# A two-layer decoder trunk on one core: where the overflow test stands, and how the last expert's last products are cut, gated and summed

## The chip, the core and the metric

The kernel runs on one core of a Trainium2 chip. The metric is device time in microseconds (us) of one execution; the median of several executions is compared. The core's engines are TensorE (PE in the profile; its weight loads are PEld), VectorE (DVE), ScalarE (ACT), GpSimd (POOL) and SyncE (SP). Here SP issues the weight loads, which 16 DMA engines carry out. Each engine works through its own queue of instructions in order and waits on semaphores for the others.

## The reference, cut to what matters

Two layers, each a token mixer and a channel mixer, with layer norms. 256 tokens, 1024 channels, float32. What the change touches is the last sub-layer: eight experts of width 3584, of which each token uses its best two, and the final layer norm.

```python
def moe_swiglu(x, w_router, w_gate_up, w_down):
    logits = (x @ w_router).astype(jnp.float32)
    top_v, top_i = lax.top_k(logits, TOP_K)
    gates = jax.nn.softmax(top_v, axis=-1)
    combine = jnp.sum(jax.nn.one_hot(top_i, N_EXPERTS, dtype=jnp.float32) * gates[..., None], axis=-2)
    y = jnp.zeros_like(x)
    for e in range(N_EXPERTS):
        y = y + combine[..., e:e + 1].astype(x.dtype) * swiglu(x, w_gate_up[e], w_down[e])
    return y
...
h = layer_norm(DEEPNORM_ALPHA * h + f, ln_ffn_g[l], ln_ffn_b[l])
```

## The kernel before

**Places and slots.** Only the rows that an expert really gets are computed. The experts are ordered by their load at run time (place 0 has the most tokens), and each place has a fixed number of slots: `SLOTS = [192, 128, 128, 64, 64, 32, 32, 32]`. A place's tokens are gathered by a product with a one-hot matrix (`gather`), run through the expert as slots, and sent back to tokens by a product with the transposed one-hot matrix (`back`). The result is multiplied by the token's gate and added to `acc` (256 x 1024, as two tiles of 128 tokens), which starts as the scaled residual.

**Overflow.** If an expert gets more tokens than its place has slots, a block under `tc.If(most > 0)` (`overflow`, L1629 to L1637, which calls `rest`) computes the others. Every engine evaluates the test; with the inputs used here the block isn't entered.

**Two chains.** `big` runs places 0, 1 and 2 with weights split into a high and a low part (ACT makes `whi` at L433, DVE `wlo` at L434, and PE multiplies in the fast fp32r format). `small` runs places 7, 6, 5, 4, 3 with raw fp32 weights, several slot groups side by side in the PE array (`Packed`). `merge` interleaves the two chains' steps by the counts in `MERGE`; the loop over `both_chains()` counts the steps as `n` and does other things at given steps. Each expert has up steps (gate and up projections) and then down steps. A down step of the small chain takes two loads of 1 MB, each with two k tiles of 128 rows by 1024 columns.

**Loads.** `slot` takes the next of `RING = 8` buffers of 1 MB and issues the load on SP (L389). SP's queue is in order, so a load waits for its buffer to be free, and all later loads wait behind it. `value_load` (L1515) reads an expert's number into a register of SP.

**The end before.** The last expert is place 3 (64 slots; the 128 rows of a bank hold two halves of 64, each a partial sum over different columns or k tiles). In its down steps (`plain_job.downs`), at `i == BRANCH` (2), six loads (`LEAD`) are issued ahead, then the overflow test is made, then the rest follows. Of its last two 1 MB loads, the left 512 columns of both come as one load and the right 512 columns as two of half the size. `last` (L219 to L251) multiplies them, copies the slot sums from PSUM with ACT (`last_y`, L216), sends them back to tokens in fp32 in four banks, and for each bank DVE multiplies by the gate and adds to `acc` (L238) and takes statistics (L514). PE's order there is written out by hand. Then DVE alone makes the final norm: mean and variance (L1590), the inverse root in small steps (L520 to L527) with four cells of 512 columns normalised between them (L1599), four last steps of 512 columns (L1601), each followed by its output DMA (L1602).

PSUM has eight banks here: four `mm`, two `tp`, two `aux`. Instructions of ACT, DVE and SP are ordered by the framework's own simulated timeline unless an order is written out, and it can't move anything into or across the block of the overflow test.

Of the kernel before, what the change touches and what calls it, by code (L numbers as in the profile page):

```python
# [23 lines left out]
NE = 8  # L24
# [55 lines left out]
class Packed:  # L80
# [5 lines left out]
    half = [slice(0, 64), slice(64, 128)]  # L86
# [126 lines left out]
    def last_y(self, bank):  # L213

        y = self.b.pp.tile([128, 512], F32, name="y", tag="gfar", bufs=3)
        self.nc.scalar.activation(y, bank, AF.Copy)  # L216
        return y

    def last(self, keys, ws, st):  # L219


        nc, b, half = self.nc, self.b, self.half
        back = b.got[self.name][1].bitcast(F32)
        y = self.last_y(self.dn)
        bks = [[b.mm_bank() for _ in range(2)] for _ in range(2)]
        for t in range(2):
            b.in_turn([(bks[h][t], back[half[h], t * 128:(t + 1) * 128], y[half[h]], True, False) for h in range(2)])

        def products(x, ks, w, first, last):
            out = []  # L230
            for i, (r, _, j) in enumerate(ks):
                out += self.times([(x[half[i % 2]], 512 * i, 512)], self.hid[r, j], w, first and i < 2, last and i >= len(ks) - 2)
            b.in_turn(out, [w.load])

        def give(h, t, y):
            cs = slice(h * 512, h * 512 + 512)
            b.mm(bks[h][t], back[:, t * 128:(t + 1) * 128], y, False, True)
            nc.vector.scalar_tensor_tensor(self.acc[t][:, cs], bks[h][t], self.gates[t][:, self.place:self.place + 1], self.acc[t][:, cs],  # L238
                                           op0=OP.mult, op1=OP.add)
            b.ln_stats(self.acc[t], st[t], h)  # L240
        with b.tc.manual_schedule(engines={mybir.EngineType.PE}):
            xs = [b.aux_bank() for _ in range(2)]
            products(xs[0], keys, ws[0], True, True)
            y0 = self.last_y(xs[0])
            products(xs[1], keys[:2], ws[1], True, False)
            give(0, 0, y0)
            products(xs[1], keys[2:], ws[2], False, True)
            y1 = self.last_y(xs[1])
            give(0, 1, y0)
            for t in range(2):  # L250
                give(1, t, y1)  # L251

    def end(self):
        nc, half = self.nc, self.half
# [15 lines left out]
class Body:  # L270
# [942 lines left out]
    def gather(self, h, wants, bank, hot=None):  # L1213
# [3 lines left out]
        nc = self.nc  # L1217
# [5 lines left out]
        xs, cols, at = [], [], 0  # L1223
# [219 lines left out]
    def plain_job(self, wg, wd, tile, tail, ready=()):  # L1443

        def ups():
            for p, (c, m) in enumerate(WIDE):
                for k in range(0, KT, 2):
                    ks = (k, k + 1)
                    tile.up(p, ks, [ready[p, i] if (p, i) in ready else self.slot(wg(i, 1, 512 * c, 512 * m)) for i in ks])
                    self.flush()  # L1450
                    self.settle()
                    yield 1

        def downs():
            loads = tile.downs()
            ends = 11 if tail else 13
            keys = loads[12] + loads[13]
            ready = {}
            for i in range(0, ends + 1, 2):
                if tail and i == BRANCH:  # L1460
                    ready = {n: self.slot(wd(loads[n])) for n in range(i, i + LEAD)}
                    self.branch()
                ws = [ready[n] if n in ready else self.slot(wd(loads[n])) for n in (i, i + 1)]
                tile.go([y for n, w in enumerate(ws) for y in tile.down(loads[i + n], w, i + n == 0, i + n == ends)],
                        [w.load for w in ws])
                if i == 12:
                    self.settling.append(tile.end)
                self.flush()
                self.settle()
                yield 1  # L1470
            if tail:
                late = [self.slot(wd(keys, 0, 512))] + [self.slot(wd(loads[n], 512, 512)) for n in (12, 13)]
                tile.last(keys, late, self.last_st)
                yield 1
        return ups(), downs()

    def moe(self, ctx, h, routing, g, b):
# [21 lines left out]
        acc = []  # L1499
        gates = []  # L1500
        eid = {}
        self.got, self.beside, self.settling = {}, [], []

        groups = {6: [("6", 6, 0, 32), ("5", 5, 0, 32), ("4", 4, 0, 64), ("3", 3, 0, 64)]}
        for place in (1, 2):
            groups[place] = [(str(place), place, 0, 128)]

        def chain(places, banks):

            for k, place in enumerate(places):  # L1510
                if place == 7:
                    eid[place] = FIXED
                else:
                    with tc.issue_after(self.loaded.ins):
                        eid[place] = nc.sync.value_load(eidi[0:1, place:place + 1], min_val=0, max_val=NE - 1)  # L1515
                name = str(place)
                if place < 3:
                    side = None
# [39 lines left out]
        for n, z in enumerate(both_chains()):  # L1558
            if n == 6:
                both, overi, mxi = next(routing)  # L1560
                gates += both
            if n == 70:
                early, (most,) = nc.values_load_multi_w_load_instructions(mxi[0:1, 0:1], min_val=-S, max_val=S)
                order = ctx.enter_context(ExitStack())
                for x in early:
                    if x.ins.engine in (mybir.EngineType.DVE, mybir.EngineType.Activation):
                        order.enter_context(tc.issue_after(x.ins))
                def branch():
                    while self.put_off:
                        self.flush()  # L1570
                    self.overflow(h, gates, overi, most, weights, eid, acc)
                self.branch = branch
                self.last_st = [self.ln_tile() for _ in range(2)]
            if n == 72:
# [10 lines left out]
        cells = [(t, hf, slice(hf * 512, hf * 512 + 512)) for t in range(2) for hf in range(2)]  # L1585
        with tc.manual_schedule(engines={mybir.EngineType.DVE}):
            mvs = []
            for st in self.last_st:
# [3 lines left out]
            ves = [self.keep.tile([128, 1], F32, name="ln_ve") for _ in mvs]  # L1592
            for mv, ve in zip(mvs, ves):
                nc.vector.tensor_scalar(ve, mv[:, 1:2], EPS, None, op0=OP.add)  # L1594
            todo = list(cells)
            for n, rs in enumerate(zip(*[self.rsqrt_steps(ve) for ve in ves])):
                if n > 0 and todo:
                    t, hf, cs = todo.pop(0)
                    nc.vector.scalar_tensor_tensor(acc[t][:, cs], acc[t][:, cs], mvs[t][:, 0:1], gb[0][hf], op0=OP.subtract, op1=OP.mult)  # L1599
            for t, hf, cs in cells:  # L1600
                nc.vector.scalar_tensor_tensor(acc[t][:, cs], acc[t][:, cs], rs[t], gb[1][hf], op0=OP.mult, op1=OP.add)  # L1601
                nc.sync.dma_start(a["out"][t * 128:(t + 1) * 128, cs], acc[t][:, cs])  # L1602

    def spread_rows(self, g, b):

# [33 lines left out]
    def rest(self, h, pos, gates, w, place, base, acc):  # L1639
# [5 lines left out]
        for t in range(2):  # L1645
# [5 lines left out]
        back = self.wk.tile([128, 256], F32, name="o_back", tag="backb", bufs=2)  # L1651
        nc.vector.tensor_copy(back, hb[:, :256])
        xT = self.hgran("o_xT")
        for q in range(2):
            bk = self.mm_bank()
            for i in range(4):
# [127 lines left out]
```

## Time and profile before

| what | value |
|---|---|
| median of 3 runs | 1458.78 us (1456.9 to 1459.31) |
| profiled execution | 1457.71 us, its span 1456.0 us |
| PE busy | 1398.4 us (96%) |
| DVE busy | 815.1 us (56%) |
| ACT busy | 658.6 us (45%) |
| DMA | 453.42 MB, mean 311 GB/s |
| mean granted PE clock | 0.991 |

Busy times are shares of the whole span; the stages differ. The attention and dense part runs to about 620 us, the expert stage from there to the end. The profile's stretches show for a part of the span how long each engine was busy, how much of the time the 16 DMA engines were at work (the DMA share, 1.00 when all are) and what they moved. The chain of waits follows the work that ended last back from the last instruction. "L304" is the one line that issues nearly every product, so products are told apart by the tiles: `aux<-raw,eh` are the small chain's downs, `mm<-y,back` the sending back to tokens.

### The profile page before, as it was taken

How to read it: one execution, taken by the hardware profiler on the slowest of the kernel's cores; microseconds unless marked ns; L12 is line 12 of the kernel's file. 1: busy time of each engine (PE TensorE's matmuls, PEld its weight loads, DVE VectorE, ACT ScalarE, POOL GpSimd, SP SyncE). 2: the span in 40 equal slices, each digit the busy share in tenths (PEclk: the TensorE clock that was granted, in tenths of full speed). 3: DMA queues.
4: the chain of work that ended last, by engine and by line, in shares of the span. 5: the costliest groups of instructions: out<-in, count | busy, mean ns of one | idle time of the engine just before them, and what ended most of it. 6: DMA issues, size and time to landing. Idle time of an engine off the chain costs nothing. (4 is left out here: it accounts for less than half of the span.)

```text
span 1456.0 us, 20149 instructions
## 1 busy us (share of the span) xinstructions
PE 1398.4 (96%) x7601; PEld 929.9 (64%) x7601; DVE 815.1 (56%) x1238; ACT 658.6 (45%) x958; POOL 16.9 (1%) x44
## 2 busy tenths in 40 slices
PE   9999999999999999999999999999999999999985
PEld 6878978888888789745544554366676555445531
DVE  7757776665586677624243443377667435344423
ACT  5656536664366664134333332256656434323310
POOL 4000000000000000000000000000000000000000
PEclk9999999999999999999999999999999999999998
DMA  9643545555385347699999999999999999999984
GB/s 299 220 132 129 176 154 194 190 172 191 113 262 172 116 135 297 257 365 401 408 417 415 414 419 421 421 420 418 418 420 420 420 420 410 420 420 420 419 352 191
DMA packets 135766, 453.42 MB, mean 311 GB/s; under 512 B 8078, under 2 KB 63398, under 8 KB 108012
## 3 DMA queue, kind: packets, MB, share of 16 engines
q1 hardware_dynamic: 134872, 450.99, 79.7%
q0 software_dynamic: 784, 1.05, 0.4%
q8 instruction: 62, 1.02, 0.3%
q14 instruction: 44, 0.36, 0.1%
q10 hardware_dynamic: 4, 0.01, 0.0%
HBM read 450.96 MB, written 1.05 MB: 310 GB/s over the span
## 5 line engine op out<-in xcount | busy, mean ns | idle before, releaser
L434 DVE TENSOR_TENSOR wlo<-raw,whi 128x1024 fp32r<-128x1024 f32 (+2 forms) x456 | 516.3, 1161 | 416.6 <-ACT whi L433 405.7
L433 ACT ACTIVATE whi<-raw 128x1024 fp32r<-128x1024 f32 (+2 forms) x456 | 441.9, 1005 | 396.2 <-DMA raw<-in_w_expert_gate_up 156.4
L304 PE MATMUL mm<-hT,whi 128*128 128x512 f32 x672 | 234.8, 399 | 0.0
L304 PE MATMUL aux<-raw,xs 128*32 128x512 f32 (+3 forms) x1280 | 185.8, 549 | 4.6 <-DMA raw<-in_w_expert_gate_up 4.6
L304 PE MATMUL mm<-hT,wlo 128*128 128x256 f32 x672 | 175.8, 281 | 0.0
L304 PE MATMUL mm<-whi,xh 128*128 128x512 f32 x336 | 140.0, 417 | 4.0 <-ACT whi L433 3.5
L304 PEld LDWEIGHTS mm<-hT,whi 128*128 128x128 f32 x672 | 121.5, 188 | 23.7 <-issue 0.7
L304 PEld LDWEIGHTS mm<-hT,wlo 128*128 128x128 f32 x672 | 126.9, 189 | 9.1 <-issue 2.0
L304 PE MATMUL mm<-whi,xl 128*128 128x512 f32 x336 | 132.7, 395 | 0.0
L304 PEld LDWEIGHTS aux<-raw,xs 128*32 128x32 f32 (+1 forms) x1280 | 57.1, 121 | 106.2 <-issue 97.7
L304 PE MATMUL aux<-raw,eh 128*32 128x512 f32 (+1 forms) x560 | 93.9, 608 | 11.8 <-DMA raw<-in_w_expert_down 8.2
L304 PE MATMUL mm<-wlo,xh 128*128 128x512 f32 x336 | 97.9, 399 | 0.8 <-DVE wlo L434 0.7
L304 PEld LDWEIGHTS mm<-whi,xh 128*128 128x128 f32 x336 | 63.2, 188 | 54.4 <-ACT whi L433 23.8
L304 PE MATMUL mm<-whi,eh 128*128 128x512 f32 x336 | 88.5, 404 | 5.0 <-ACT whi L433 4.9
L304 PEld LDWEIGHTS mm<-whi,eh 128*128 128x128 f32 x336 | 60.0, 188 | 36.0 <-ACT whi L433 19.7
L304 PEld LDWEIGHTS mm<-wlo,xh 128*128 128x128 f32 x336 | 61.6, 188 | 20.9 <-DVE wlo L434 4.1
L304 PEld LDWEIGHTS mm<-whi,xl 128*128 128x128 f32 x336 | 63.2, 188 | 11.6
L304 PEld LDWEIGHTS aux<-raw,eh 128*32 128x32 f32 (+1 forms) x560 | 26.3, 122 | 62.1 <-issue 59.1
L429 ACT ACTIVATE sums<-mm 128x512 f32<-128x512 f32 x84 | 50.3, 602 | 32.0 <-PE mm L304 30.7
L304 PE MATMUL aux<-hT,whi 128*128 128x512 f32 x160 | 56.3, 396 | 0.0
L304 PE MATMUL mm<-raw,xs 128*64 128x512 f32 x224 | 54.2, 605 | 0.0
L304 PE MATMUL mm<-whi,hT 128*128 128x260 f32 (+2 forms) x192 | 51.4, 336 | 2.1 <-DVE hT L434 1.1
(348 smaller groups left out, 1614.8 us busy)
## 6 DMA issues: line engine op xcount, KB each, us to landing
raw<-in_w_expert_gate_up SPq DMA_DIRECT2D x140, 1024.0 KB, 12.8
raw<-in_w_expert_down SPq DMA_DIRECT2D x111, 1024.0 KB, 13.1
raw<-in_w_expert_gate_up SPq DMA_DIRECT2D x112, 768.0 KB, 12.1
raw<-in_w_in SPq DMA_DIRECT2D x36, 1024.0 KB, 5.3
raw<-in_w_ffn_gate_up SPq DMA_DIRECT2D x22, 1024.0 KB, 5.0
raw<-in_w_ffn_down SPq DMA_DIRECT2D x10, 1024.0 KB, 4.9
raw<-in_w_out SPq DMA_DIRECT2D x8, 1024.0 KB, 5.0
raw<-in_w_in SPq DMA_DIRECT2D x8, 520.0 KB, 7.3
```

The source lines that it names most:

```text
L304: self.made = self.nc.tensor.matmul(out, lhsT, rhs, start=start, stop=stop)
L429: self.nc.scalar.activation(x, bank, AF.Copy, scale=scale)
L433: return (self.nc.scalar.activation(hi, src, AF.Copy), self.nc.vector.tensor_sub(lo, src, hi.bitcast(F32)))
L434: self.nc.vector.tensor_sub(lo, src, hi.bitcast(F32)))
```

## The change

1. The overflow test leaves the last expert's downs. It is made once at step `n == 96`, which is the last step of the largest expert (place 0), after everything put off has been flushed. The lead loads go. All expert numbers are read into registers at step 60, and the largest overflow at step 60 in place of 70. Inside the block, which isn't entered, some buffers come from other pools.
2. For the last expert, the last eight k tiles (four loads) are loaded in six pieces: left 512 columns of four k tiles, left 512 of the other four, right 512 of the first four in two loads, and the right 512 of the last four in two loads of 256 columns. From `i == 4` on, each load's products wait for that load alone.
3. `seed` (new) copies the right half of `acc` and puts it by products with the identity into two PSUM banks, so that the token sums are added there. All four `mm` banks hold token sums; the slot sums of the last pieces have `aux` and `tp` banks.
4. The gate is gathered for each slot (`slot_gate`) and applied by ACT when the slot sums are copied (`gated`, new), with a low part by DVE for all pieces but the last, so that the sums go back in fp32r in two steps; the last piece goes back in fp32.
5. Statistics are taken over 256 columns at a time. The right half is normalised straight from PSUM. The final norm has six cells in its first step (two of 512, four of 256) and four of 512 in its second, as before.

```diff
-BRANCH, LEAD = 2, 6
-MERGE = ((42, 47), (50, 14), (42, 46))
+MERGE = ((42, 47), (50, 14), (42, 45))
+BRANCH, LAST = 96, "3"
...
+    def seed(self):
+        b = self.b
+        self.sums = [[b.mm_bank() for _ in range(2)] for _ in range(2)]
+        for n, bank in enumerate(self.sums[1]):
+            x = b.pp.tile([128, 512], F32, name="seed", tag="silu", bufs=4)
+            c = 512 + 256 * n
+            for t in range(2):
+                self.nc.scalar.activation(x[:, t * 256:t * 256 + 256], self.acc[t][:, c:c + 256], AF.Copy)
+            b.mm(bank, b.ident, x, True, False)
+
+    def gated(self, hi, src, lo=None):
+        gate = self.b.slot_gate
+        self.nc.scalar.activation(hi, src, AF.Copy, scale=gate)
+        if lo is not None:
+            self.nc.vector.scalar_tensor_tensor(lo, src, gate, hi.bitcast(F32), op0=OP.mult, op1=OP.subtract)
+        return hi, lo
...
+        y = self.gated(row(), self.dn, row())
         with b.tc.manual_schedule(engines={mybir.EngineType.PE}):
+            x = b.aux_bank()
+            products([(x, 0, 512, 512)], keys[:4], ws[0], True, False)
+            out = []
+            for i, z in enumerate(y):
+                for t, s in enumerate((a0, a1)):
+                    out.append((s, back[half[0], cols[t]], z[half[0]], i == 0, False))
+                    out += [(s[:, two[t]], back[half[1], cols[t]], z[half[1]][:, two[n]], False, False) for n, s in enumerate((sb, sc))]
+            b.in_turn(out)
+            products([(x, 0, 512, 512)], keys[4:], ws[1], False, True)
+            y = self.gated(row(), x, row())
+            xs = [b.tp_bank() for _ in two]
+            both = [(xs[n], 256 * n, 256, 512) for n in range(2)]
+            products(both, keys[:2], ws[2], True, False)
+            products(both, keys[2:4], ws[3], False, False)
+            b.in_turn([(s, back[:, cols[t]], z, False, i == 1) for t, s in enumerate((a0, a1)) for i, z in enumerate(y)])
+            for t, s in enumerate((a0, a1)):
+                nc.vector.tensor_add(self.acc[t][:, :512], s, self.acc[t][:, :512])
+                for c in range(2):
+                    nc.vector.bn_stats(out=st[t][:, c], in_=self.acc[t][:, two[c]])
+            products([(xs[0], 0, 256, 256)], keys[4:], ws[4], False, True)
+            y = self.gated(far(F32R), xs[0][:, :256], far(F32R))
+            products([(xs[1], 0, 256, 256)], keys[4:], ws[5], False, True)
+            b.in_turn([(sb[:, two[t]], back[:, cols[t]], z, False, t == 1 and i == 1) for t in range(2) for i, z in enumerate(y)])
+            y = self.gated(far(F32), xs[1][:, :256])[0]
+            b.in_turn([(sc[:, two[t]], back[:, cols[t]].bitcast(F32), y, False, t == 1) for t in range(2)])
+            for n, s in enumerate((sb, sc)):
+                for t in range(2):
+                    nc.vector.bn_stats(out=st[t][:, 2 + n], in_=s[:, two[t]])
...
+            if name == LAST:
+                for t in range(2):
+                    self.mm(tb[:, 256:257], rows[t], self.gates[t][:, place:place + 1], t == 0, t == 1)
+                self.slot_gate = self.wk.tile([128, 1], F32, name="slot_gate", bufs=1)
+                nc.vector.tensor_copy(self.slot_gate, tb[:, 256:257])
...
-            ends = 11 if tail else 13
+            ends = 9 if tail else 13
             for i in range(0, ends + 1, 2):
-                if tail and i == BRANCH:
-                    ready = {n: self.slot(wd(loads[n])) for n in range(i, i + LEAD)}
-                    self.branch()
-                ws = [ready[n] if n in ready else self.slot(wd(loads[n])) for n in (i, i + 1)]
+                ws = [self.slot(wd(loads[n])) for n in (i, i + 1)]
+                made = [tile.down(loads[i + n], w, i + n == 0, i + n == ends) for n, w in enumerate(ws)]
+                if tail and i >= 4:
+                    for y, w in zip(made, ws):
+                        tile.go(y, [w.load])
...
+                if tail and i == 4:
+                    tile.seed()
...
+                first, last = (loads[n] + loads[n + 1] for n in (10, 12))
+                late = [self.slot(wd(keys, c0, n)) for keys, c0, n in
+                        ((first, 0, 512), (last, 0, 512), (first[:2], 512, 512), (first[2:], 512, 512), (last, 512, 256), (last, 768, 256))]
...
-            if n == 70:
+            if n == 60:
+                for place in range(NE):
+                    expert(place)
                 early, (most,) = nc.values_load_multi_w_load_instructions(mxi[0:1, 0:1], min_val=-S, max_val=S)
...
+            if n == BRANCH:
+                while self.put_off:
+                    self.flush()
+                self.overflow(h, gates, overi, most, weights, eid, acc)
...
-            todo = list(cells)
+            todo = list(self.sums)
             for n, rs in enumerate(zip(*[self.rsqrt_steps(ve) for ve in ves])):
                 if n > 0 and todo:
-                    t, hf, cs = todo.pop(0)
-                    nc.vector.scalar_tensor_tensor(acc[t][:, cs], acc[t][:, cs], mvs[t][:, 0:1], gb[0][hf], op0=OP.subtract, op1=OP.mult)
+                    t, cs, src = todo.pop(0)
+                    hf = cs.start // 512
+                    nc.vector.scalar_tensor_tensor(acc[t][:, cs], src, mvs[t][:, 0:1], gb[0][hf][:, cs.start - 512 * hf:cs.stop - 512 * hf], op0=OP.subtract, op1=OP.mult)
```

More of the change, by code (lines that the diff above doesn't have):

```diff
@@ L226, in last, with row, far @@
-        for t in range(2):
-            b.in_turn([(bks[h][t], back[half[h], t * 128:(t + 1) * 128], y[half[h]], True, False) for h in range(2)])
-        def products(x, ks, w, first, last):
+        back = b.got[self.name][1]
+        cols = [slice(t * 128, t * 128 + 128) for t in range(2)]
+        two = [slice(t * 256, t * 256 + 256) for t in range(2)]
+        (a0, a1), (sb, sc) = self.sums
+        def row():
+            return b.row_tile("y", F32R)
+        def far(dt):
+            return b.pp.tile([128, 512], dt, name="y", tag="gfar", bufs=3)[:, :256]
@@ L230, in products @@
+        def products(outs, ks, w, first, last):
             out = []
             for i, (r, _, j) in enumerate(ks):
-                out += self.times([(x[half[i % 2]], 512 * i, 512)], self.hid[r, j], w, first and i < 2, last and i >= len(ks) - 2)
+                for x, c0, n, size in outs:
+                    out += self.times([(x[half[i % 2]][:, :n], size * i + c0, n)], self.hid[r, j], w, first and i < 2, last and i >= len(ks) - 2)
             b.in_turn(out, [w.load])
[L235 to L240, printed above, removed]
@@ L241, in last @@
-        with b.tc.manual_schedule(engines={mybir.EngineType.PE}):
[L242 to L251, printed above, removed]
+        y = self.gated(row(), self.dn, row())
@@ L253, in end @@
+        return [(t, slice(0, 512), self.acc[t][:, :512]) for t in range(2)] + [
+            (t, slice(512 + 256 * n, 768 + 256 * n), s[:, two[t]]) for n, s in enumerate((sb, sc)) for t in range(2)]
     def end(self):
@@ L1455, in downs @@
             loads = tile.downs()
-            ends = 11 if tail else 13
-            keys = loads[12] + loads[13]
-            ready = {}
+            ends = 9 if tail else 13
             for i in range(0, ends + 1, 2):
-                if tail and i == BRANCH:
-                    ready = {n: self.slot(wd(loads[n])) for n in range(i, i + LEAD)}
-                    self.branch()
-                ws = [ready[n] if n in ready else self.slot(wd(loads[n])) for n in (i, i + 1)]
-                tile.go([y for n, w in enumerate(ws) for y in tile.down(loads[i + n], w, i + n == 0, i + n == ends)],
-                        [w.load for w in ws])
+                ws = [self.slot(wd(loads[n])) for n in (i, i + 1)]
[3 more added lines that the diff above has]
+                        tile.go(y, [w.load])
+                else:
+                    tile.go(made[0] + made[1], [w.load for w in ws])
                 if i == 12:
@@ L1469, in downs @@
                 self.settle()
+                if tail and i == 4:
+                    tile.seed()
                 yield 1
             if tail:
-                late = [self.slot(wd(keys, 0, 512))] + [self.slot(wd(loads[n], 512, 512)) for n in (12, 13)]
-                tile.last(keys, late, self.last_st)
+                first, last = (loads[n] + loads[n + 1] for n in (10, 12))
+                late = [self.slot(wd(keys, c0, n)) for keys, c0, n in
+                        ((first, 0, 512), (last, 0, 512), (first[:2], 512, 512), (first[2:], 512, 512), (last, 512, 256), (last, 768, 256))]
+                self.sums = tile.last(first + last, late, self.last_st)
                 yield 1
@@ L1506, in moe, with expert @@
             groups[place] = [(str(place), place, 0, 128)]
+        def expert(place):
+            if place == 7:
+                eid[place] = FIXED
+            elif place not in eid:
+                with tc.issue_after(self.loaded.ins):
+                    eid[place] = nc.sync.value_load(eidi[0:1, place:place + 1], min_val=0, max_val=NE - 1)
         def chain(places, banks):
             for k, place in enumerate(places):
[L1511 to L1515, printed above, removed]
+                expert(place)
                 name = str(place)
@@ L1561, in moe @@
                 gates += both
-            if n == 70:
+            if n == 60:
+                for place in range(NE):
+                    expert(place)
                 early, (most,) = nc.values_load_multi_w_load_instructions(mxi[0:1, 0:1], min_val=-S, max_val=S)
@@ L1567, in moe @@
                         order.enter_context(tc.issue_after(x.ins))
[L1568 to L1574, printed above, removed]
+                self.last_st = [self.keep.tile([128, 4, 6], F32, name="last_st", bufs=2) for _ in range(2)]
+            if n == 62:
                 order.close()
+            if n == BRANCH:
+                while self.put_off:
+                    self.flush()
+                self.overflow(h, gates, overi, most, weights, eid, acc)
             if n == 160:
@@ L1594, in moe @@
                 nc.vector.tensor_scalar(ve, mv[:, 1:2], EPS, None, op0=OP.add)
-            todo = list(cells)
+            todo = list(self.sums)
             for n, rs in enumerate(zip(*[self.rsqrt_steps(ve) for ve in ves])):
                 if n > 0 and todo:
-                    t, hf, cs = todo.pop(0)
[L1599 to L1602, printed above, removed]
+                    t, cs, src = todo.pop(0)
+                    hf = cs.start // 512
+                    nc.vector.scalar_tensor_tensor(acc[t][:, cs], src, mvs[t][:, 0:1], gb[0][hf][:, cs.start - 512 * hf:cs.stop - 512 * hf], op0=OP.subtract, op1=OP.mult)
+            for hf in range(2):
+                for t in range(2):
+                    cs = slice(hf * 512, hf * 512 + 512)
+                    nc.vector.scalar_tensor_tensor(acc[t][:, cs], acc[t][:, cs], rs[t], gb[1][hf], op0=OP.mult, op1=OP.add)
+                    nc.sync.dma_start(a["out"][t * 128:(t + 1) * 128, cs], acc[t][:, cs])
     def spread_rows(self, g, b):
@@ L1650, in rest @@
             hot.append(x)
[L1651 removed]
+        back = self.row_tile("o_back")[:, :256]
         nc.vector.tensor_copy(back, hb[:, :256])
[L1653 removed]
+        xT = self.pp.tile([128, 1024], F32, name="o_xT", tag="whi", bufs=4)
         for q in range(2):
```

10 lines of the change are left out of this document (1 added, 9 removed).

## The prediction

> **What bounds the kernel now.** I read the page first, then the busy time by stretches, then what surrounds the overflow test, then the chain that ended last. The expert stage runs from about 640 us to the end. Its columns below are stretch, its length, busy time of PE, PEld, DVE, ACT, POOL (with counts), granted PE clock, DMA share, GB/s.
>
> ```profile
> raw<-in_w_expert_down SPq DMA_DIRECT2D x111, 1024.0 KB, 13.1
> 1300.00:1400.00 100.00, 96.16 (x445) 51.21 (x444) 42.36 (x42) 35.36 (x41) 0.00 (x0) 1.00 1.01 419
> ```
>
> The DMA engines are never free here: share 1.01 at 419 GB/s, so 1 MB (1.05 million bytes) every 2.5 us, and a load lands 13.1 us after its issue, so some five loads are under way at any time. PE is near its limit too (96%), but the DMA engines have no idle time and PE has some. So the end of the stage is the bytes over 419 GB/s, plus every hole in the stream, plus what comes after the last byte. Both of the last two are what the change touches.
>
> The hole is at the overflow test (L1632):
>
> ```profile
> L1632 SPq EVENT_SEMAPHORE  x9: 17/17/17, 1405.1 to 1416.8; - x9
> L1632 SPq COMPARE_BRANCH  x1: 53/53/53, 1399.9 to 1399.9; - x1
> L1632 PEldq COMPARE_BRANCH  x1: 6191/6191/6191, 1404.1 to 1404.1; - x1
> SPq L1632 <- SPq L1632: 16.6, 6, 5.2
> PE aux L304 <- PEq L1632: 3.7, 1, 3.7
> 1417.06 5.50 SPq L389 DMA_DIRECT2D raw<-in_w_expert_down  x7
> ```
>
> SP compares at 1399.9 and then steps through nine semaphores until 1416.8. They stand for what the skipped block would have counted, the loads' own semaphores among them, and each of those is passed only when the loads issued on it have landed. So the test drains the stream, however many loads were issued ahead of it; the six "lead" loads filled those 17 us and no more. The next seven loads go out from 1417.06 on. What that costs stands in the stretches:
>
> ```profile
> 1406.00:1408.00 2.00, 1.08 (x8) 0.80 (x6) 0.00 (x0) 0.87 (x2) 0.00 (x0) 1.00 1.02 410
> 1408.00:1410.00 2.00, 0.00 (x0) 0.00 (x0) 0.00 (x0) 0.00 (x0) 0.00 (x0) 0.80 0.99 401
> 1410.00:1412.00 2.00, 1.26 (x4) 0.59 (x6) 0.00 (x0) 0.00 (x0) 0.00 (x0) 0.50 0.77 307
> 1412.00:1414.00 2.00, 2.00 (x6) 0.53 (x4) 0.00 (x0) 0.00 (x0) 0.00 (x0) 0.50 0.53 213
> 1414.00:1416.00 2.00, 2.00 (x8) 0.65 (x6) 0.00 (x0) 0.00 (x0) 0.00 (x0) 0.50 0.18 74
> 1416.00:1418.00 2.00, 2.00 (x12) 0.74 (x10) 0.00 (x0) 0.00 (x0) 0.00 (x0) 0.99 0.00 0
> 1418.00:1420.00 2.00, 2.00 (x12) 0.78 (x10) 0.00 (x0) 0.00 (x0) 0.00 (x0) 1.00 1.03 307
> ...
> 1430.00:1432.00 2.00, 2.00 (x11) 0.72 (x10) 0.00 (x0) 0.00 (x0) 0.00 (x0) 1.00 1.05 389
> 1432.00:1434.00 2.00, 2.00 (x12) 0.85 (x10) 0.00 (x0) 0.49 (x1) 0.00 (x0) 1.00 1.03 376
> 1434.00:1436.00 2.00, 2.00 (x10) 0.67 (x8) 0.00 (x0) 0.70 (x2) 0.00 (x0) 1.00 0.03 9
> ```
>
> Two things are to be seen. First the size: against 419 GB/s the rows from 1408 to 1416 lack 18+112+206+345 = 681, times 2 us over 419 = 3.25 us; those from 1416 to 1420 lack 419+112 = 531, or 2.55 us. Hole: 5.8 us. Second its shape: the 3.25 us are **ragged**. The share falls over six us (0.99, 0.77, 0.53, 0.18), so some DMA engines were done long before the one that lands last; in 700 us without a pause they had drifted apart. The 2.55 us are dead time of the restart. At 1434, 16 us after a restart, the stream ends sharply (1.03, then 0.03). So a drain costs its raggedness, and it also sets the engines level for the next end.
>
> After the last byte, at 1434.0, come 22 us:
>
> ```profile
> 1418.86 10.82 DMA raw<-in_w_expert_down
> 1429.68 0.14 issue
> 1429.82 5.37 PE aux L304 x24
> 1435.19 1.92 PE mm L304 x8
> 1437.11 1.01 PE aux L304 x4
> 1438.12 1.05 PE mm L304 x2
> 1439.17 1.01 PE aux L304 x4
> 1440.18 1.07 PE mm L304 x2
> 1441.25 0.03 issue
> 1441.27 0.76 DVE acc L238
> 1442.04 0.02 issue
> 1442.06 0.69 DVE ln_st L514
> 1442.76 1.31 DVE acc L238 x2
> 1444.06 1.19 DVE ln_st L514 x2
> 1445.26 0.24 DVE ln_mv L1590 x2
> ...
> 1446.00 0.66 DVE acc L1599
> ```
>
> PE waits for a pair of loads until 1429.68 and is then itself the bound for 11.4 us; the last byte (1434.0) waits for PE, not PE for it. Then DVE sums, takes statistics until 1445.26, and normalises; the page's span ends at 1456.0, 10.75 us after the statistics.
>
> **The change, part by part.**
>
> *The overflow test goes from the last expert's second pair of down loads to the step after the largest expert.* Its place in time:
>
> ```profile
> L1419 DVE SCALAR_TENSOR_TENSOR acc<-tp,gate,acc x12: 742/744/752, 953.3 to 1402.7; 128x512 f32<-128x512 f32 x12
> ```
>
> The largest expert's sums begin at 953.3, so the test falls at about 957. SP still stops there until all it has issued has landed, and every later load is queued behind it. The stream is as full there as later, so the drain isn't removed; it is moved. Its dead part I take as before, 2.55 us. Its ragged part is unknown at 957: 0 at the least (sharp, as at 1434), 3.25 at the most (as at 1410); the stream has then run 300 us rather than 750, but 16 us of sharpness is much farther off, so I take 2.4. Mid-stage hole: 4.95, bounds 2.55 to 5.8. In exchange the stream now runs 450 us without a drain up to the kernel's end, so it ends ragged: again 2.4, bounds 0 and 3.25, where before it was 0. Together -5.8 + 4.95 + 2.4 = **+1.55 us**, bounds -3.25 and +3.25. So moving the test alone gains nothing by my account.
>
> PE, ACT and DVE pass the test too. PE's compare took 6.19 us, of which 3.7 were idle, with six loads waiting in the ring. Without lead loads PE now consumes everything, flushes the largest expert's put-off sums, and only then jumps. Meanwhile SP has refilled the ring: eight slots are 20 us of stream, more than the jump, so SP isn't held up for long. I put +0.5 us for it, bounds 0 and 2. The register loads for all experts at step 60 and the maximum's load moved from step 70 to 60 stand on SP with five loads under way: nothing.
>
> *The last eight k tiles in column pieces.* The bytes are the same, in six loads (two of 1 MB, four of half) in place of two whole 1 MB loads and three pieces. Rows of 8 KB run at 419 GB/s; the rows of 1430 to 1434, which by the code are those with 2 KB runs, at (389+376)/2 = 383. So 2 KB runs cost 0.23 us for each 1.05 million bytes, and there is 1 MB more of them: +0.25. The last 1 MB has 1 KB runs, which this trace doesn't show in a full stream; at a fixed cost for each run the loss against 8 KB doubles and more: +0.55, bounds 0.23 and 1.0. Together **+0.8 us**.
>
> [...]
>
> *Seed.* Four ACT copies and two fp32 products with the identity, 1.07 us each by the chain (1440.18), 2.1 us on PE. They are hidden in the small expert's downs:
>
> ```profile
> 1424.80 3.65 PE L304 MATMUL aux<-raw,eh 128*64 128x512 f32 x16 [0.93 <-DMA raw<-in_w_expert_down]
> 1389.31 1.16 PE L304 MATMUL mm<-wlo,eh 128*128 128x512 f32 x4
> 1440.23 0.60 ACT L216 ACTIVATE y<-aux 128x512 f32<-128x512 f32 x1 [4.41 <-PE aux L304]
> ```
>
> Two loads take PE 3.65 us and DMA 5.0, so 0.67 us is free at each load and four loads cover it; uncovered it would be 2.1. The gate's two small products and its copy lie 600 us before the end: nothing.
>
> *The tail.* Let T be the last byte. The pieces land at about T-8.5, -5.8, -4.4, -3.0, -1.5 and T, plus 0.85 for the semaphore (bytes gone before 1416, SP through at 1416.8). PE's work ahead of the last piece: the two 1 MB pieces 1.83 each, the two halves together 1.83, the first sums (four steps of fp32r at 1.16/4 = 0.29, with two halves of 64 rows side by side as at 1435.19, where four such fp32 products took 1.92 and not 4 x 1.07) 1.2, the second sums 4 x 0.29 = 1.2, the next-to-last piece 0.9: 8.8 us in the 8.5 there are. So PE arrives about level with the last piece; if halves don't run side by side it is 1.2 us or more late. Then: semaphore 0.85, products on 256 columns of four k tiles (half the 1.83 and the pipe's end) 1.0, gated copy of 256 columns 0.5 (0.60 for 512), two fp32 sums of 256 columns 1.07, last statistics 0.55: T+3.95. On DVE two adds, eight statistics of 256 columns and one low part must fit between, some 5 us from about T-0.3 on, so I add 0.7: statistics end at **T+4.65**, bounds 3.95 and 6.4. Before it was 1445.26 - 1434.0 = T+11.25. After that the 10.75 us stay, but six cells in place of four are normalised, two of 0.66 and four of about 0.4 against four of 0.66: +0.3. This part gains 11.25 - 4.65 - 0.3 = **6.3 us**.
>
> *Sum:* 6.3 - 1.55 - 0.5 - 0.8 = 3.45 us. On the profiled execution: T becomes 1434.0 + 2.85 = 1436.85, the span 1436.85 + 4.65 + 11.05 = 1452.55, its time 1457.71 - 3.45 = 1454.3. That execution lies 1.07 under the median of the runs shown, so I forecast 1458.78 - 3.45 = **1455.3 us**.
>
> **Rivals.**
>
> *A. The stream ends sharply.* If the engines don't drift in 450 us, the end's 2.4 falls away, and the gain is 5.85: 1452.9 us. For: 16 us after a restart they are level. Against: they were far apart at 1410.
>
> *B. Full raggedness at both drains and a late PE.* Ragged 3.25 twice gives +3.25 rather than +1.55, and the tail T+5.0: gain 1.4, 1457.4 us, no change to be measured. For: drift may be quick to saturate. Against: nothing in the trace.
>
> *C, the other side. PE, not the stream, pays for the new place.* Behind the largest expert no load lies in the ring when PE jumps. PE's stop: ACT's and DVE's work on the sums and PE's eight products some 5 us, the jump 6.2, the first load's split 2.4: 13.6 us, and then half clock (0.50 in the rows from 1410 to 1416, so 3 us lost). That is 16.6 where the sum has 4.95 and 0.5. If PE has no slack afterwards, 11.15 us more is lost: 1455.3 + 11.15 = 1466.5 us. It decides if PE's backlog, nearly seven loads, holds so many of the eight slots that the stream starves, and PE catches up at no more than its 4% idle time. For: 96% busy. Against: the ring's 20 us cover 16.6, and 450 us at 4% give 18 us back.
>
> [...]
>
> *D. The drain vanishes at the new place,* because SP finds all landed: 4.95 more, 1450.4 us. Against: SP's issue always runs five loads ahead.
>
> **How the numbers follow.** My forecast 0.40, A 0.20, B 0.28, C 0.09, D 0.03. A measurement here can tell about 0.2%, 2.9 us. Forecast, A and D lie beyond that, but the forecast only by 0.5 us, so I leave a ninth of its chance to no change: faster 0.58. Same: 0.28 + 0.05, or 0.33. Slower 0.09. The range leaves out C and D and reaches past A and B by the run-to-run spread of some 1.5 us: 1451.0 to 1460.0. The bounds of all terms would allow about 1449 to 1461.
>
> **What would show it.** Right: at about 957 to 985 a stretch in which SP's nine semaphores take 13 to 18 us and the DMA share falls to 0; from there to the end no other fall; a last stretch in which the share falls over 3 us or more; statistics ending 4 to 6 us after the last byte and the span 11 us after these. Wrong: a share under 0.97 for tens of us after the test (C); a sharp end (A); PE without a gap for more than 5 us after the last byte, or DVE's low parts queued behind the statistics. The forecast falls if the time is over 1458 or under 1451.

## The result and the profile after

The changed kernel takes 1449.6 us in the median (1449.24 to 1452.09), the kernel before 1457.24 us (1456.52 to 1459.31): a ratio of 0.9947, 95% interval 0.9934 to 0.996. It is faster by 7.6 us where 3.45 were forecast, and the time lies below the predicted range of 1451 to 1460. The profiled execution of after is 1449.29 us, its span 1447.6.

The first row to hold against the prediction's is the stretch of the full stream, far from anything that the change touches. Columns as there: stretch, length, busy time of PE, PEld, DVE, ACT, POOL, granted PE clock, DMA share, GB/s.

```profile
1300.00:1400.00 100.00, 96.19 (x447) 51.37 (x446) 43.68 (x45) 33.65 (x39) 0.00 (x0) 1.00 1.01 426
```

The DMA share is 1.01 as before, PE is as busy as before, but the engines move 426 GB/s and not 419. Nothing in the diff is meant to touch these loads. Over the 790 us of the expert stage 7 in 419, or 1.7%, is some 13 us, more than the whole gain; so something else must have lost time.

It was lost at the overflow test, which is now at L1681. First the instructions of that line in after (times in ns min/median/max, then first and last start in us), then SP's own waits from 920 to 990 us, then what SP issued there.

```profile
L1681 SPq EVENT_SEMAPHORE  x9: 17/17/17, 949.5 to 950.1; - x9
L1681 SPq COMPARE_BRANCH  x1: 53/53/53, 946.6 to 946.6; - x1
L1681 PEldq COMPARE_BRANCH  x1: 6172/6172/6172, 953.2 to 953.2; - x1
```

```profile
SPq L1664 <- PE mm L338: 16.4, 1, 16.4
SPq L1681 <- SPq L1681: 2.8, 1, 2.8
```

```profile
924.95 4.87 SPq L423 DMA_DIRECT2D raw<-in_w_expert_gate_up  x2
946.31 0.26 SPq L1664 DMA_DIRECT2D ln_gb<-in_ln_ffn_b  x1
950.29 4.42 SPq L423 DMA_DIRECT2D raw<-in_w_expert_gate_up  x8
```

The picture differs from the test before. There SP compared and then stood among its nine semaphores for 12 us. Here it passes them within 0.6 us, because all had landed before: SP had issued no weight load since about 930, and the DMA share in the rows below is 0.00 from 942 on. It stood 16.4 us on one small load, the last quarter of the final norm's gain and bias (`ln_gb`, L1664), whose buffer PE's products still held. All that follows in SP's queue, the test included, stood behind it. The stretches of after show the hole that this tore:

```profile
938.00:942.00 4.00, 4.00 (x21) 2.47 (x18) 2.79 (x3) 2.60 (x3) 0.00 (x0) 1.00 0.44 181
942.00:946.00 4.00, 4.00 (x29) 1.38 (x27) 1.29 (x2) 1.08 (x2) 0.00 (x0) 1.00 0.00 0
946.00:950.00 4.00, 2.69 (x10) 1.27 (x8) 2.83 (x5) 0.60 (x1) 0.00 (x0) 1.00 0.02 7
950.00:954.00 4.00, 2.52 (x8) 0.95 (x8) 2.80 (x5) 0.00 (x0) 0.00 (x0) 0.89 0.64 207
954.00:958.00 4.00, 0.00 (x0) 0.00 (x0) 0.61 (x1) 0.00 (x0) 0.00 (x0) 0.50 1.02 423
```

The missing shares, 0.56 + 1.00 + 0.98 + 0.36, times 4 us are 11.6 us without transfers. Then comes PE's own jump: busy 0.00 and clock 0.50 while the stream is already full again.

The tail of after, as stretches and as the end of its chain of waits (start, length, what):

```profile
1424.00:1426.00 2.00, 2.00 (x11) 0.68 (x11) 0.75 (x1) 0.00 (x0) 0.00 (x0) 1.00 1.05 407
1426.00:1428.00 2.00, 2.00 (x18) 1.22 (x18) 0.00 (x0) 0.00 (x0) 0.00 (x0) 1.00 1.08 392
1428.00:1430.00 2.00, 2.00 (x18) 1.31 (x16) 0.43 (x1) 0.69 (x1) 0.00 (x0) 1.00 0.72 249
1430.00:1432.00 2.00, 2.00 (x14) 1.09 (x12) 1.04 (x3) 0.00 (x0) 0.00 (x0) 1.00 0.08 28
1432.00:1434.00 2.00, 1.91 (x17) 0.96 (x13) 2.00 (x6) 0.83 (x2) 0.00 (x0) 1.00 0.00 0
```

```profile
1409.73 14.00 DMA raw<-in_w_expert_down
1423.86 1.94 PE aux L338 x8
1425.80 1.14 PE mm L338 x8
1426.94 1.87 PE aux L338 x8
1428.81 1.78 PE tp L338 x16
1430.59 0.68 PE mm L338 x2
1431.29 1.29 DVE acc L272 x2
1432.58 1.31 DVE last_st L274 x4
1433.89 0.39 DVE y L230
1434.33 1.50 PE mm L338 x7
1435.85 0.76 DVE last_st L283 x2
1437.41 0.66 DVE acc L1646
```

PE waits last for a load at 1423.86 and works without a gap until the last pieces' products are done; then the chain is DVE's. The fall of the share ends between 1430 and 1432, and the statistics end at 1436.6 (1435.85 + 0.76), against 1434.0 and 1445.26 before.

### The profile page after: what moved, and what is told of

Same layout as the page of the kernel before. It is cut to its first block, busy times and chain, and to the rows that moved or that the text cites. A ratio compares the mean times of both kernels' runs of the same rounds, so it can differ in the third digit from the quotient of the medians.

```text
span 1447.6 us, 20217 instructions
## 1 busy us (share of the span) xinstructions
PE 1390.9 (96%) x7633; PEld 933.2 (64%) x7633; DVE 816.3 (56%) x1246; ACT 659.2 (46%) x963; POOL 16.9 (1%) x44
## 5 line engine op out<-in xcount | busy, mean ns | idle before, releaser
L338 PE MATMUL mm<-whi,xh 128*128 128x512 f32 x336 | 140.1, 417 | 11.8 <-ACT whi L467 11.7
L338 PE MATMUL aux<-raw,eh 128*32 128x512 f32 (+1 forms) x544 | 87.9, 598 | 5.7 <-DMA raw<-in_w_expert_down 5.6
```

Of the source, the lines that this page charges most:

```text
L338: self.made = self.nc.tensor.matmul(out, lhsT, rhs, start=start, stop=stop)
```

## The experiments

After the result there were two theories on the rate. P: the rate hangs on where in SBUF the weight buffers begin. The new statistics tiles (`last_st`, 2 x 96 bytes for each partition) are placed ahead of the weight ring and push it on. Read from the compiled programs (the profiles show no addresses), the ring begins here (byte in a partition):

```
before  raw ring at 22848  (64 past a multiple of 256)
after   raw ring at 23040  (a multiple of 256 and of 512)
```

The rival is that the rate came with the change itself, by its order of work. For the rest, the question was how the test's new place and the tail share what the rate does not explain.

**The ring moved by a pad.** Before, plus one unused tile of 192 bytes, so that the ring begins at 23040; all that is allocated behind the tile moves with it:

```diff
+        nc.vector.memset(self.keep.tile([128, 48], F32, name="pad", bufs=1), 0.0)
```

> The kernel before with one unused tile of 192 bytes a partition beside the statistics, and nothing else: all weight buffers move from byte 22848 of a partition to 23040, that is from 64 past a multiple of 256 to a multiple of 512. Theory P (the place of the buffers sets the DMA rate): 426 GB/s in place of 419 in the middle of the expert stage, and 12 to 13 us less than before, about 1444 us. Theory Q (the rate differs by chip, or by the order of the work): 419 GB/s and the time of before, about 1457.

Measured: 1444.66 us (1444.05 to 1446.46) against 1457.04 for before, run along with it, ratio 0.9913 [0.9897, 0.993]; from 1300 to 1390 us its loads run at 425 GB/s. A tile that nobody reads makes the old kernel 12.4 us faster, and 5 us faster than the changed one. P holds, and the rival (419 GB/s and some 1457 us) falls.

**The change without it.** After, plus 64 bytes, so that the ring begins at 23104, again 64 past a multiple of 256:

```diff
+        nc.vector.memset(self.keep.tile([128, 16], F32, name="pad", bufs=1), 0.0)
```

> The changed kernel with one unused tile of 64 bytes, so that the weight buffers begin 64 past a multiple of 256 again, as before the change (23104). P: the stream falls back to 419 GB/s and the time rises by about 12 us to 1461 or 1462, slower than before the change, since the mid-stage hole of 11.6 us stays. Q: 426 GB/s and 1449.6 us as changed.

Measured: 1461.92 us (1461.26 to 1462.32), ratio 1.0034 [1.0021, 1.0046]; from 1300 to 1390 us its loads run at 420 GB/s. What the change does by intention makes the kernel 4.9 us **slower**; the 192 bytes that came with it make it faster.

**Which multiple.** Before with 448 bytes (ring at 23296, a multiple of 256 but not of 512) and with 64 bytes (22912, 128 past one):

```diff
+        nc.vector.memset(self.keep.tile([128, 112], F32, name="pad", bufs=1), 0.0)
...
+        nc.vector.memset(self.keep.tile([128, 16], F32, name="pad", bufs=1), 0.0)
```

> The kernel before with an unused tile of 448 bytes: weight buffers at 23296, a multiple of 256 but not of 512. If 256 bytes is the step that counts: 426 GB/s and about 1444.7 us as with 192 bytes. If it is 512: 419 GB/s and about 1457.

> The kernel before with an unused tile of 64 bytes: weight buffers at 22912, 128 past a multiple of 256. If 256 is the step: 419 GB/s or less and 1457 us or a little more. If 64 or 128 bytes were enough: 426 GB/s and 1444.7.

Measured: 1445.96 us (two runs, 0.992 [0.9901, 0.994]) and 1456.73 us (0.9993 [0.9983, 1.0003]). The same stretch of the padded kernels, first 448 bytes (at 23296), then 64 bytes (at 22912):

```profile
1300.00:1400.00 100.00, 92.48 (x430) 49.16 (x428) 40.27 (x39) 32.50 (x39) 0.00 (x0) 1.00 1.01 425
```

```profile
1300.00:1400.00 100.00, 96.26 (x446) 51.32 (x444) 42.46 (x43) 35.25 (x41) 0.00 (x0) 1.00 1.01 419
```

Of the places tried, the two at a multiple of 256 (23040, 23296) gave 425 to 426 GB/s, those 64 past one (22848, 23104) 419 to 420, and the one 128 past (22912) 419: 512 isn't needed, 128 isn't enough. That it is the ring's place, and not that of another tile behind the pad, is argued and not shown: in after, the queue of these loads moves 38.26 of the 38.34 MB from 1300 to 1390 us.

**The move alone.** The kernel with 192 bytes, and of the change only the new place of the test, with no lead loads (the tail as before); the register loads at step 60 and the other buffers inside the skipped block go with it:

```diff
-BRANCH, LEAD = 2, 6
+BRANCH = 96
...
-                if tail and i == BRANCH:
-                    ready = {n: self.slot(wd(loads[n])) for n in range(i, i + LEAD)}
-                    self.branch()
...
+            if n == BRANCH:
+                while self.put_off:
+                    self.flush()
+                self.overflow(h, gates, overi, most, weights, eid, acc)
```

> The kernel before, padded by 192 bytes as in the first run, with only the move of the overflow test: behind the largest expert, without lead loads, all expert numbers read at step 60. Additive account: against the padded kernel the old place's hole (4.7 us there) goes, one of 11.6 us comes, and the end is ragged, 1 to 2 us: 1444.7 + 7 to 9, about 1452 to 1454. Rival (the move is worth something by itself, and the fast stream hides it): 1444.7 or less.

Measured: 1453.58 us (1452.39 to 1455.41), ratio 0.9974 [0.9962, 0.9985], which is 8.9 us over the padded kernel. Moving the test is a loss of that size, and SP's wait is the same as in after:

```profile
SPq L1618 <- PE mm L304: 16.4, 1, 16.4
```

**The tail alone.** After with the test back among the last expert's downs, with its six lead loads; ring at 23040:

```diff
-BRANCH, LAST = 96, "3"
+BRANCH, LEAD, LAST = 2, 6, "3"
...
+                if tail and i == BRANCH:
+                    ready = {n: self.slot(wd(loads[n])) for n in range(i, i + LEAD)}
+                    self.branch()
```

> The changed kernel with the overflow test back in the last expert's downs and six loads issued ahead of it, as before; buffers at 23040 as in the changed kernel. Forecast's account (moving the test gains nothing by itself, the tail's pieces gain about 5): 12.5 from the rate and 5 from the tail, about 1439 to 1441, and 8 to 10 us below the changed kernel. Rival (the test was the costly part at the old place, as the change's order suggests): no better than the changed kernel, 1449 or more.

Measured: 1440.72 us (1439.45 to 1441.97), ratio 0.9889 [0.9872, 0.9905]: 3.9 us better than the padded kernel, and of all kernels that still make the test the fastest, 8.9 us ahead of the changed one. Its hole, with the test at the old place:

```profile
1396.00:1398.00 2.00, 2.00 (x3) 0.50 (x2) 0.00 (x0) 0.92 (x3) 0.00 (x0) 0.54 0.96 397
1398.00:1400.00 2.00, 2.00 (x4) 0.67 (x2) 0.00 (x0) 0.00 (x0) 0.00 (x0) 0.61 0.93 377
1400.00:1402.00 2.00, 2.00 (x9) 0.63 (x10) 0.00 (x0) 0.00 (x0) 0.00 (x0) 1.00 0.47 197
1402.00:1404.00 2.00, 2.00 (x12) 0.71 (x10) 0.00 (x0) 0.00 (x0) 0.00 (x0) 1.00 0.03 12
1404.00:1406.00 2.00, 2.00 (x12) 0.70 (x10) 0.00 (x0) 0.00 (x0) 0.00 (x0) 1.00 0.82 201
```

(0.04 + 0.07 + 0.53 + 0.97 + 0.18) x 2 = 3.6 us.

**The test taken out.** To price the test itself, both places without the block (the tokens over an expert's slots are left out):

```diff
-                self.overflow(h, gates, overi, most, weights, eid, acc)
```

> The changed kernel without the overflow block (the part of the computation that is left out: the tokens over an expert's slots, of which there are none with these inputs); the largest expert's put-off sums are still flushed at the same step. Theory H, what the test costs at its new place is the stretch without loads and nothing else: 1449.6 - 11.6 = 1438. Rival N, PE has no slack behind the test and works off a backlog that the stop left, so its price is more than the stretch: 1435 or less. Rival L, the stop gave PE time that it needs anyway, or the undisturbed stream ends more ragged, so that less comes back: 1441 or more.

> The kernel with the new tail and the test at its old place (e4_tail), without the overflow block (the same part is left out); its six lead loads stay. Theory H: the hole in the stream there sums up to about 3.7 us, so 1440.7 - 3.7 = 1437, and within 1.5 us of the other kernel of this call, since both are then the same program but for the counts of the merge. Prediction's price of the old place, 5.8 us less a ragged end of 2.4: 1437.3 as well, so it does not tell these apart. Rival Z, the test costs nothing at the old place since PE sets the end there: 1440 to 1441.

Measured: 1437.85 us (1437.46 to 1438.26) and 1437.36 us (1436.27 to 1437.89). The two floors differ in the lead loads and in where the put-off sums are flushed (the counts of `MERGE` are the same in both), and they agree within 0.5 us; so the difference between after and the tail alone is the test. The test costs 1449.6 - 1437.85 = 11.8 us at its new place, where the hole is 11.6, and 1440.72 - 1437.36 = 3.4 at the old one, where it is 3.6. With the new tail, the stretch without transfers is the price in both places (theory H).

Two things limit this. Counted by bytes against 426 GB/s, in place of shares, the rows shown lack 12.3 and 4.4 us, since the first loads behind the stop moved little at a high share (0.82 at 201 GB/s). And with the old tail the holes are not all: the padded kernel's sums to 5.0 us by shares (1398 to 1408), that of the move alone to 11.0 (938 to 954), which is 6.0 more, while the medians differ by 8.9 and the profiled executions by 7.1.

**The small load behind the test.** After, with the gain's and bias's loads held back until the last issued weight load:

```diff
-                nc.sync.dma_start(x[0:1], row[None, hf * 512:(hf + 1) * 512])
+                with self.tc.issue_after(self.loaded.ins):
+                    nc.sync.dma_start(x[0:1], row[None, hf * 512:(hf + 1) * 512])
```

> The changed kernel with the four small loads of the last norm's gain and bias issued behind the weight load that is the latest when the step is written, so none stands ahead of the overflow test. Theory L (SP's 16.4 us wait for the last of them makes half of the hole): the hole in the stream at the test shrinks from 11.6 to 5 to 6 us, as at the old place, and the time falls by some 6 us to 1443 or 1444. Rival: the ring has to refill in any case and PE is the bound behind the test; then the hole stays at 10 us or more, or the time stays within 2 us of 1449.6.

Measured: 1445.43 us (1444.91 to 1448.31), ratio 0.9926 [0.991, 0.9943]: 4.2 us back of the 6 expected. The hole is smaller, and a second one is new:

```profile
938.00:942.00 4.00, 4.00 (x22) 2.21 (x19) 2.87 (x3) 2.60 (x3) 0.00 (x0) 1.00 0.62 252
942.00:946.00 4.00, 4.00 (x29) 1.84 (x29) 1.47 (x3) 1.09 (x2) 0.00 (x0) 1.00 0.55 170
...
954.00:958.00 4.00, 0.73 (x3) 0.02 (x1) 1.41 (x2) 0.00 (x0) 0.00 (x0) 0.50 1.02 427
958.00:962.00 4.00, 0.47 (x1) 0.47 (x2) 0.48 (x1) 1.57 (x2) 0.00 (x0) 0.50 0.96 391
962.00:966.00 4.00, 4.00 (x12) 2.88 (x11) 4.00 (x4) 4.00 (x5) 0.00 (x0) 0.64 0.33 77
```

```profile
SPq L423 <- DVE wlo L468: 24.7, 5, 16.2
```

The drain proper is (0.38 + 0.45) x 4 = 3.3 us. Then the stream is full while PE, ACT and DVE pass the test and consume little or nothing; the ring of eight fills up, SP waits 16.2 us for DVE to free a buffer, and at 962 the engines run dry: (0.04 + 0.67) x 4 = 2.8 us. The kernel without the test shows nothing of either in the same place:

```profile
942.00:946.00 4.00, 4.00 (x29) 2.27 (x29) 2.21 (x3) 1.64 (x4) 0.00 (x0) 1.00 1.00 420
946.00:950.00 4.00, 4.00 (x18) 2.24 (x17) 2.73 (x4) 2.42 (x3) 0.00 (x0) 1.00 1.03 429
```

So 4.2 of the 11.8 us were the small load's, and of the 7.6 that stay, the drain and the starved ring show 6.1 by shares; by bytes they lack 4.0 and 4.2 us (with 358 GB/s from 966 to 970), 8.2 together.

**All loads ahead of the test.** The tail alone, with the test behind the issue of all of the last loads, so that no load has to wait for it, and with the seed behind the test:

```diff
-BRANCH, LEAD, LAST = 2, 6, "3"
+BRANCH, LAST = 8, "3"
...
-                    ready = {n: self.slot(wd(loads[n])) for n in range(i, i + LEAD)}
+                    ready = {n: self.slot(wd(loads[n])) for n in (i, i + 1)}
+                    first, last = (loads[n] + loads[n + 1] for n in (10, 12))
+                    late = [self.slot(wd(keys, c0, n)) for keys, c0, n in
+                            ((first, 0, 512), (last, 0, 512), (first[:2], 512, 512), (first[2:], 512, 512), (last, 512, 256), (last, 768, 256))]
...
-                if tail and i == 4:
+                if tail and i == BRANCH:
                     tile.seed()
```

> The changed kernel with the overflow test in the last expert's downs as late as can be: the last eight loads are all issued, then the test, and the seed behind it. No load stands behind the test, so the drain costs nothing in the stream. Theory: the 4 us hole of the run with the old place goes, PE's jump of 6 us is partly paid since eight loads remain and each leaves PE 0.6 us: 1437 to 1439, 2 to 4 us below that run's 1440.7. Rival: the jumps of PE and ACT stand uncovered so near the end: 1441 to 1444.

Measured: 1450.34 us (1448.11 to 1451.59), ratio 0.9949 [0.9933, 0.9966]; both expectations missed. The stream has no hole, and the loss is PE's:

```profile
1406.00:1408.00 2.00, 0.00 (x0) 0.00 (x0) 0.00 (x0) 0.00 (x0) 0.00 (x0) 1.00 1.01 409
1408.00:1410.00 2.00, 0.00 (x0) 0.00 (x0) 0.00 (x0) 0.00 (x0) 0.00 (x0) 0.56 1.04 394
1410.00:1412.00 2.00, 0.00 (x0) 0.00 (x0) 0.00 (x0) 1.30 (x4) 0.00 (x0) 0.50 1.05 408
1412.00:1414.00 2.00, 0.00 (x0) 0.00 (x0) 0.00 (x0) 0.04 (x1) 0.00 (x0) 0.50 1.07 407
1414.00:1416.00 2.00, 0.00 (x0) 0.00 (x0) 0.00 (x0) 0.00 (x0) 0.00 (x0) 0.50 1.02 367
1416.00:1418.00 2.00, 1.97 (x2) 0.50 (x2) 0.00 (x0) 0.00 (x0) 0.00 (x0) 0.50 0.69 243
```

```profile
ACT seed L222 <- PEq L1686: 19.7, 1, 19.7
PE mm L338 <- issue: 10.2, 1, 10.2
```

Some ten us of standing PE weren't caught up in the 13 us of stream that were left. PE's jump (5.96 us from 1404.5) was over by 1410.8 and ACT's seed copies were done by 1412.1 (1.30 from 1410, 0.04 after); why PE stood until 1416 all the same isn't shown, and the profile names only its own issue. Against the floor the test costs 13.0 us there.

## Why the prediction was right or wrong

The measured parts add up. Before to after is -12.4 (rate) + 8.4 to 8.9 (move: 11.8 - 3.4, or the move alone) - 3.9 (tail) = -7.9 to -7.4; measured -7.6. The 8.4 is taken from after and the tail alone themselves, so with it the sum closes nearly by itself; the 8.9 comes from a kernel of its own. The change with its ring 64 past a multiple is +4.9, against 8.4 to 8.9 - 3.9 = 4.5 to 5.0.

**The rate.** The step that failed is "The bytes are the same ... Rows of 8 KB run at 419 GB/s": the rate of before was taken over for after, with no bound, and it was one of this kernel's layout. It went to 426 GB/s, and the pad shows it to be worth 12.4 us, more than the whole gain. That `last_st` gets tiles of its own, ahead of the weight ring, was not considered at all. The runs gave 425/419, or 1.4%, to 426/419, or 1.7%. In these runs it is the written SBUF side that was moved, and that the step lies at 256 is shown by the runs at 128 past (419 GB/s) and at 256 (425). Why the loads are slower off a multiple of 256 is not shown.

**The old hole, -5.8, and the ragged end, +2.4.** The runs don't price these two apart. Taking the test out at the old place gave 3.4 us (the ranges of both kernels allow 1.6 to 5.7), the move alone points to about 3 with the old tail (11.8 - 8.9), and the prediction's price of that place, 5.8 less 2.4, is 3.4 as well. In the tail alone the hole is 3.6 us by shares, which leaves the ragged end 0.2, or 4.4 by bytes, as the prediction counted, which leaves 1.0 (the prediction's own rows lack 5.1 us by shares). The shape was as foretold. In after, with no restart shortly before it, the stream ended over some three us: the share is 0.95, 0.81, 0.63, 0.48, 0.22 and 0.07 in steps of half a us from 1428. In the tail alone, 16 us behind a restart, it ended sooner: 1.04, 0.48 and 0.01 in the rows of two us from 1418. That the DMA engines drift apart in a long stream was the author's reading; the rows give only the mean share of all 16. What a ragged end costs stays open: in after PE is what the end waits for, and with the old tail 2.4 to 2.9 us of the move lie beyond the holes (1.1 between the profiled executions).

**The new hole, +4.95.** Its mechanism was as told: SP stops, the stream drains. The drain itself, 3.3 us with the small load out of the way, is inside the bounds of 2.55 to 5.8. But this place was mis-sized most: 4.95 here and 0.5 for PE were foretold and 11.8 measured, while the old place and the end together came out as priced. What failed is "The register loads ... stand on SP with five loads under way: nothing": the register loads were looked at, the four `ln_gb` loads were not, though they are on SP's queue at this very point. In SP's timeline of before the last of them stands behind ten weight loads more, and goes out without a stop:

```profile
932.24 20.48 SPq L389 DMA_DIRECT2D raw<-in_w_expert_gate_up  x10
952.76 0.32 SPq L1615 DMA_DIRECT2D ln_gb<-in_ln_ffn_b  x1
955.84 32.47 SPq L389 DMA_DIRECT2D raw<-in_w_expert_gate_up  x15
```

With the test as a barrier it could not stand behind those loads, went directly ahead of the test, and stood 16.4 us. Holding it back gave 4.2 us.

**PE behind the test, +0.5 (0 to 2).** Mis-sized: some 2.8 us show as the second hole when the small load is out of the way. The text "eight slots are 20 us of stream, more than the jump, so SP isn't held up for long" is what fell: the engines did not jump at once. In that kernel ACT compares at 946.9, PE at 954.2 and DVE at 954.8; PE is 6.07 us in its jump, ACT waits for it, and splitting begins anew at 960.4, with PE's granted clock at 0.50. SP waits 16.2 us for a buffer. This is rival C, at a price of about 3 us (4 by bytes) and not of 11. Its condition, a backlog that fills the ring, is what one sees there; in after itself no second hole shows (1.00 and 1.01 from 958 to 966), for the ring had stood empty.

**The tail, -6.3 + 0.8.** 5.5 foretold, 3.9 measured; the two kernels' times (1444.05 to 1446.46 and 1439.45 to 1441.97) allow 2.1 to 7.0, so the term isn't refuted. Its structure holds: PE arrives about level with the last piece, the span ends 11.0 us after the statistics (1447.6 - 1436.6; 11.05 foretold). In steps of half a us the share is 0.03 from 1431.0 and 0.00 from 1431.5, so the statistics end some 5 us after the last byte, against 4.65. What is late is what the last part named: DVE's low part (1433.89) is queued behind four statistics that start at 1432.58, and PE's last seven products wait for it until 1434.33. The 0.8 was on the high side: the stretches that by the code move rows of 2 KB and then of 1 KB ran at 407 and 392 GB/s in after, against 426. By these rates one MB more of each costs 0.1 and 0.2 us, 0.3 together (an estimate).

**Rivals and range.** A and B differ from the forecast mainly by the raggedness of the end, whose price the runs leave open. D, "SP finds all landed", came true to the letter, and was the costliest case rather than the cheapest: SP found all landed because it had long stopped issuing. The forecast's direction was right by an accident of layout: on its own terms (+2.05 for the move, -5.5 for the tail) it had the tail about right and the move 6.5 us too cheap, and the intended change is slower (by 4.9 us with the ring where it had been).

## What to carry to other kernels

Before costing a change, look at what it does to addresses: one small tile in a pool ahead of a DMA ring can move all of its buffers off or onto a multiple of 256 bytes, here 12.4 us of 1457, and an unused pad of 192 bytes is the cheapest gain in this study. The conditional block that every engine has to evaluate was a barrier for the order of work, and SP stood 16.4 us ahead of it on one small load: list all that can be on the issuing queue just ahead of it, the small loads with busy buffers first. The price of a drained stream was the time without transfers, to about one us, in the kernels with the new tail, where the stream is the bound. The test was cheapest where six loads had been issued ahead of it (3.4 us); it cost 11.8 in the middle of a full ring, 4.2 of them by the small load, and 13.0 behind the issue of the last loads, where PE stood for ten of the last 13 us of the stream.

## What the runs showed of the hardware

- Weight loads of 1 MB and 768 KB into SBUF, from 1300 to 1390 us: 419 to 420 GB/s with the buffers 64 or 128 bytes past a multiple of 256, 425 to 426 at a multiple of 256, with the DMA share at 1.01 in both. The share therefore didn't tell the slower full stream from the faster one.
- The jump over the skipped block took PE 6.17 us in after, 6.19 in before, 6.07 with the small load held back, 5.91 in the tail alone and 5.96 with all loads ahead of the test. Behind it the granted clock stayed at 0.50 while PE worked again: for 5.3 us in before (1410.7 to 1416.0) and for about 6 in after (from 960.7) and in the kernel with all loads ahead of the test (from 1416.0).
- How sharply the stream of loads ended differed with what stood before it. In after its share fell over some three us (0.95 to 0.03 in steps of half a us from 1428 to 1431.5). In both kernels without the test it fell over two rows of two us: 0.64 and 0.08 from 1416 with the order of after, 0.74 and 0.22 from 1414 with that of the tail alone. Where it had restarted 16 us earlier, it was 0.99, 0.10 and 0.00 in steps of half a us from 1433.5 (before), and 0.48 and 0.01 in rows of two us from 1420 (the tail alone).
